# Spreading the state-space convolutions over linear-attention heads and gates, with deeper rings of decays

## The chip, the cores and the metric

The kernel runs on one core of one Trainium2 chip. The metric is the device time of one execution in microseconds (us). PE is the matrix engine, DVE the vector engine, ACT the scalar engine (it evaluates functions such as Exp, Ln and Silu and has to load a table of functions before it can use one that is not in the table it holds), POOL the third elementwise engine, and SP the queue from which most DMA transfers are issued. A verdict on this kernel can tell a change of about 0.2% from none, which is 4.9 us.

## The reference

Two layers of a hybrid encoder trunk on 512 tokens of width 1024, in float32. Each layer projects the normalised input with one wide matrix and feeds three mixers, whose outputs are gated and added:

```python
xbc = silu(dwconv_centred(xbc, conv_w, conv_b))          # 5 taps over the tokens: xs (1024), B and C (2 groups x 128)
y_f = ssd_chunked(xs, dtf, -exp(a_log_f), Bm, Cm)        # decay = exp(tril(a_i - a_j)), 16 heads of 64, chunks of 128
y_b = rev(ssd_chunked(rev(xs), rev(dtb), -exp(a_log_b), rev(Bm), rev(Cm)))
y   = rms_grouped((y_f + y_b + xs * d) * silu(z)) * norm_w
...
g_f = log_sigmoid(ga_f @ a2_f + bias_f) / 16             # linear attention: 4 heads, keys 128, values 256
o   = gla_chunked(q, k, v, g_f) + rev(gla_chunked(rev(q), rev(k), rev(v), rev(g_b)))
...
mixed = sig(gate0) * (y @ Ws) + sig(gate1) * (o @ Wg) + sig(gate2) * (na @ Wn)
x = x + mixed @ w_out;   x = x + relu(rms(x) @ w_ff1)^2 @ w_ff2
```

## The kernel before

All weights come as 128x1024 tiles, called granules here. For each granule SP issues a DMA into `wr`, ACT rounds it into a high part `wh` (L285), DVE subtracts for the low part `wl` (L287), and PE makes 24 matmuls of 512 columns (L304 high x high, L305 low x high, L306 high x low, for 8 slices) into a PSUM tile `pf`; value projections use two granules and tiles `pt` of 256 columns (L321 to L323). `wr`, `wh` and `wl` have rings of three, `pf`/`pt` one of two: a granule can start only when the one of the two tiles that it is given has been read out (evacuated) by DVE or ACT. A list of weight keys fixes the order of granules, and it must be the order in which the code asks for them. Within that order a scheduler places the instructions of each engine; every engine then runs its own list strictly in order.

Each layer has these stages: neighbourhood attention (N), linear attention (G), state-space (S), then the output projection and the MLP (F). The change touches G and S.

- G, four heads. `gla_proj(h)` makes values and gates (`gvg`), `q` and `k`. `gla_mix(h)` computes the decays for two directions d: a small matmul `ga` (L667), on ACT Abs, Exp and Ln (L670, L673, L674), on POOL a subtraction (L676), on DVE a scan (L682), on ACT two Exp of the scan (L685, L686) and one of a difference (L692), on DVE products with q and k (L693 to L699), and then the score matmuls `at` on PE (L709, L712). `gla_out` transposes a head's output (L780) and splits it into `Ah` (ACT L348) and `Al` (DVE L349). Branch granules `br_1x` (weights `br`, branch 1) multiply all eight `Ah`/`Al`; gate granules `gate_1x` make sigmoid gates (evacuated by L603, then ACT L605), and the branch's evacuation multiplies into the gate tile `gl` (L617).
- A convolution, `conv_tile`, is one granule (`xs`, `B` or `C`), its evacuation into `cu` on DVE (L789), one ACT pass (L792), four DVE passes (L797), and Silu on ACT (L798). Group 0 has six (xs_0 to xs_3, B_0, C_0), made after the last head has been projected; group 1 has six more.
- S, eight pairs of heads. For each head two rows of logarithmic decays are broadcast by DMA to 128 partitions (`S_E` and `S_eB`, 256 KB each); DVE takes differences and minima (L910), ACT scales two copies (`S_T`, `S_tb`, L912, L913) and takes Exp (L915), and DVE adds and multiplies (L916, L917). PE then multiplies (L945 into `S_py`, L956). Between the steps of a pair, `fill` runs granules of a list `todo`: the group 1 convolutions, gates and branches of branch 1, then z gates.

Of the kernel before, what the change touches and what calls it, by code (L numbers as in the profile page):

```python
# [199 lines left out]
def trunk(tc, a, out, layers=L, dbg=None):  # L200
    nc = tc.nc
    V, S, G, T = nc.vector, nc.scalar, nc.gpsimd, nc.tensor
    with ExitStack() as ctx:
# [13 lines left out]
        def nm(s):  # L217
            cnt[0] += 1
            return f"{s}_{cnt[0]}"
# [13 lines left out]
        def flat(ap):  # L233
            return ap.rearrange("p a b -> p (a b)")
# [20 lines left out]
        ph = Phase(tc, "F0", F_SB, F_PS)  # L255
# [41 lines left out]
        def feat(l, key, rh, rl, ps=None):  # L297

            hi, lo = wget(l, key)
            if ps is None:  # L300
                ps = psm("pf")
            for k in range(KT):
                c = slice(P * k, P * (k + 1))
                T.matmul(ps, lhsT=hi[:, c], rhs=rh[k], start=k == 0, stop=False)  # L304
                T.matmul(ps, lhsT=hi[:, c], rhs=rl[k], start=False, stop=False)  # L305
                T.matmul(ps, lhsT=lo[:, c], rhs=rh[k], start=False, stop=k == KT - 1)  # L306
            return ps
# [74 lines left out]
        for l in range(layers):  # L382
# [7 lines left out]
            ks = [("nk", t) for t in range(8)]  # L390
            for t in range(8):
                ks += [("nq", t), ("nv", t)]
            gk_ = lambda h: [("gvg", h, i) for i in range(4)] + [("gq", h), ("gk", h)]
            bk_ = lambda b, js=range(8): [k for j in js for k in (("gate", b, j), ("br", b, j))]
            ck_ = lambda g: [("xs", 4 * g + j) for j in range(4)] + [("B", g), ("C", g)]
            ks += [("sm", 0)] + gk_(0) + bk_(0) + gk_(1) + gk_(2) + gk_(3)
            ks += ck_(0) + ck_(1) + bk_(1) + [("z", j) for j in range(8)]
            ks += [("gate", 2, j) for j in range(5)]
            for j in range(8):
                ks += [("br", 2, j)] + ([("gate", 2, j + 5)] if j < 3 else [])  # L400
# [18 lines left out]
            if l:  # L419
                for j in range(KT):  # L420
# [5 lines left out]
            ph = Phase(tc, f"N{l}", {"s": 5, "pT": 4, "va0": (1, 1152), "va1": (1, 1152), "vb0": (1, 896), "vb1": (1, 896),  # L426
# [172 lines left out]
            def gate(b, j):  # L599
                ps = feat(l, ("gate", b, j), xh, xl)  # L600
                g_ = evac("gl")
                with hp():
                    V.tensor_tensor(g_, ps, rbc, ALU.mult)  # L603
                with hp():
                    S.activation(g_, g_, AF.Tanh, scale=0.5)  # L605
                return g_

            def branch(b, j, bh, bl, g_=None):
                if g_ is None:
                    g_ = gate(b, j)  # L610
                ps = feat(l, ("br", b, j), bh, bl)
                with hp():
                    if b == 0:
                        mixed[j] = pa.tile([P, NT], F32, tag="mix", name=nm("mixed"))
                        V.scalar_tensor_tensor(mixed[j], g_, 1.0, ps, ALU.add, ALU.mult)
                    else:
                        V.scalar_tensor_tensor(g_, g_, 1.0, ps, ALU.add, ALU.mult)  # L617
                if b:
                    G.tensor_tensor(mixed[j], mixed[j], g_, ALU.add)


            px_ = Phase(tc, f"X{l}", {"xs": 4, "bc": 2}, {})
            ph = Phase(tc, f"G{l}", {"A": 1, "kwT": 2, "st0": (3, 256), "st1": (3, 256), "t1": 3, "t2": 3, "w": 2,
                                     "gvg": 8, "bs": 2, "gst": 1, "q": 1, "k": 1, "a2": (2, 256), "kx": (2, 256)},
                       {"ga": 1, "at": 1, "x": 2, "po": 2})
# [9 lines left out]
            def gla_proj(h):  # L635
                v_, g_ = [], []
                for n, (r_, fn) in enumerate(((v_, AF.Copy), (g_, AF.Silu))):
                    ps = token(l, [("gvg", h, 2 * n), ("gvg", h, 2 * n + 1)], xh, xl)
                    for i in range(2):
                        t_ = ph.t("gvg", (P, 2, 256))  # L640
                        for b in (0, 1):
                            with hp():
                                S.activation(t_[:, b], ps[i][:, 256 * b: 256 * b + 256], fn,
                                             scale=rtok[:, 2 * i + b: 2 * i + b + 1])
                        r_.append(t_)
                ps = feat(l, ("gq", h), xh, xl)
                q_ = ph.t("q")
                with hp():
                    V.scalar_tensor_tensor(q_, ps, DK ** -0.5, rbc, ALU.mult, ALU.mult)
                ps = feat(l, ("gk", h), xh, xl)  # L650
                k_ = ph.t("k")
                with hp():
                    V.tensor_tensor(k_, ps, rbc, ALU.mult)
                return q_, k_, v_, g_
# [121 lines left out]
            def gla_out(g_):  # L776
                for vh in range(2):
                    py = ph.p("x", (P, 4, P))
                    for i in range(4):
                        T.transpose(py[:, i], g_[i // 2][:, i % 2, P * vh: P * (vh + 1)], ident)  # L780
                    h_, l_ = split(flat(py), cc(C_GLAN + vh), "Ah", "Al", pa)
                    glh.append(h_)
                    gll.append(l_)

            def conv_tile(pxs, n, i, ci):
                ps = feat(l, (n, i), xh, xl)
                u = evac("cu")
                with hp():
                    V.tensor_tensor(u, ps, rbc, ALU.mult)  # L789
                o = (px_ if n == "C" else pxs).t("xs" if n == "xs" else "bc")  # L790
                w_ = lambda k: cc(C_CW + 5 * ci + k)
                S.activation(o, u, AF.Identity, bias=cc(C_CB + ci), scale=w_(2))  # L792
                for k in (0, 1, 3, 4):
                    d = k - 2
                    so = slice(max(0, -d), NT - max(0, d))
                    si = slice(max(0, d), NT - max(0, -d))
                    V.scalar_tensor_tensor(o[:, so], u[:, si], w_(k), o[:, so], ALU.mult, ALU.add)  # L797
                S.activation(o, o, AF.Silu)  # L798
                return o

            conv_list = lambda g: [("xs", 4 * g + j, 4 * g + j) for j in range(4)] + [("B", g, 8 + g), ("C", g, 10 + g)]
# [3 lines left out]
            for j in range(8):  # L805
                branch(0, j, nah, nal)
            gla_out(y0)
            cur = gla_proj(1)
            for h in range(1, 4):
                y = gla_mix(h, *cur)  # L810
                if h < 3:
                    cur = gla_proj(h + 1)
                    gla_out(y)
            c0 = [conv_tile(px_, *k) for k in conv_list(0)]
            gla_out(y)
            ph.close()


            ph = Phase(tc, f"S{l}", {"xt": 2, "bt": 1, "gs": 1, "xw": (2, 768), "st": (2, 768), "eb": 4, "E": 4, "eB": 2,
                                     "T": 2, "tb": 1, "sm": 2, "xs": 4, "bc": 1, "tm": (1, 256)},  # L820
                       {"x": 4, "py": 2})

            pdt = ph.p("x", (P, 4, 32))
# [3 lines left out]
            sm = [smt[i // 4][:, i % 4].rearrange("p (c h) -> p c h", c=4) for i in range(8)]  # L827
# [161 lines left out]
                    sdl.append(l_)  # L989


            c1, todo = [], []
            for k in conv_list(1):
                todo.append(lambda k=k: c1.append(conv_tile(ph, *k)))
            for j in range(8):
                todo.append(lambda j=j: gls.append(gate(1, j)))
                todo.append(lambda j=j: branch(1, j, glh, gll, gls.pop(0)))
            for j in range(4):
                todo.append(lambda j=j: gate_tile(0, j, c0[:4]))
            gls = []  # L1000

            def fill(n=1):
                for _ in range(min(n, len(todo))):
                    todo.pop(0)()
# [5 lines left out]
            st = pair_states(0, 0, bts[0], cur[1])  # L1010
            for n, (g, j) in enumerate(pairs):
                nxt = pairs[n + 1] if n < 7 else None
                if nxt:
                    if nxt == (1, 0):
                        bts.append(ssd_group(1, c1))
                    new = pair_prep(*nxt, cs[nxt[0]])
                fill(1 + (n > 3))
                pair_out(g, j, cs[g], cur[0], cur[2], st)
                fill(1)
                if nxt:  # L1020
                    st = pair_states(*nxt, bts[nxt[0]], new[1])
                    cur = new
                fill(1)
# [7 lines left out]
            gs = [gate(2, j) for j in range(5)]  # L1031
# [6 lines left out]
            ph = Phase(tc, f"F{l + 1}", F_SB, F_PS)  # L1038
# [47 lines left out]
```

## Time and profile before

| | us |
|---|---|
| median of 3 runs (lowest, highest) | 2444.17 (2443.42, 2446.34) |
| the profiled execution, its own time | 2445.34 |
| its span, first to last instruction | 2443.6 |
| PE busy | 2428.9 (99%) |
| DVE busy | 1435.6 (59%) |
| ACT busy | 1157.9 (47%) |
| POOL busy | 393.3 (16%) |

PE is busy nearly all the time, so a time in this kernel is the work of PE and the gaps in it. The mean granted clock was 1.000, that is the 2.4 GHz level throughout. G of layer 0 lies at about 268 to 550 us and S at 550 to 700 us; S of layer 1 lies at about 1770 to 1910 us.

### The profile page before, as it was taken

What the parts mean: (1) busy time and instruction counts of PE and PEld (TensorE: products, weight loads), DVE (VectorE), ACT (ScalarE), POOL (GpSimd) and SP (SyncE); (2) the same over time, 40 slices, a digit from 0 to 9 for tenths busy, and PEclk for the clock granted to TensorE, in tenths of its full rate; (3) what the DMA queues carried; (4) which work ended last, traced back from release to release, by engine and by line L of the source; (5) the groups of instructions that cost most, each with busy time, mean ns of one, the idle gap of its engine ahead of it and who ended that gap; (6) DMA issues with size and microseconds to landing.
All of it is one profiled execution on the core that took longest, in us unless ns stands there. A gap on an engine that the chain in (4) does not pass through costs nothing.

```text
span 2443.6 us, 32635 instructions
## 1 busy us (share of the span) xinstructions
PE 2428.9 (99%) x12656; PEld 2063.0 (84%) x12656; DVE 1435.6 (59%) x2156; ACT 1157.9 (47%) x2055; POOL 393.3 (16%) x333
## 2 busy tenths in 40 slices
PE   9999999999999999999999999999999999999999
PEld 7899889987888888888888998899888888888887
DVE  6786534587976553443457755345989665534443
ACT  4475425556855342332335754265578543422321
POOL 3132101112431210000122321011134212100000
PEclk9999999999999999999999999999999999999999
DMA  5231222224533323223333222222245332232222
GB/s 183 89 105 63 90 87 79 72 77 134 166 112 126 100 96 97 95 95 100 124 125 97 86 69 88 87 73 85 78 139 168 102 129 95 95 100 98 93 97 87
DMA packets 84603, 249.38 MB, mean 102 GB/s; under 512 B 9824, under 2 KB 15840, under 8 KB 84448
## 3 DMA queue, kind: packets, MB, share of 16 engines
q1 hardware_dynamic: 84016, 246.85, 30.8%
q8 instruction: 100, 1.64, 0.3%
q10 hardware_dynamic: 432, 0.45, 0.1%
q14 instruction: 55, 0.45, 0.1%
HBM read 242.80 MB, written 4.46 MB: 101 GB/s over the span
## 4 chain that ended last, share of the span: by engine, by line
PE 96%; DMA 1%; DVE 1%; ACT 1%; issue 0%; SPq 0%; DVEq 0%
PE pf L305 14%; PE pf L304 14%; PE pf L306 14%; PE F_pf L304 11%; PE F_pf L306 11%; PE F_pf L305 11%; PE pt L322 3%; PE pt L323 3%; PE pt L321 3%; PE N_po L580 2%; PE N_pt L570 1%; PE S_x L956 1%; PE S_py L945 1%; PE N_sc L554 1%; PE N_sc L555 1%; PE G_x L743 1%
## 5 line engine op out<-in xcount | busy, mean ns | idle before, releaser
L285 ACT ACTIVATE wh<-wr 128x1024 fp32r<-128x1024 f32 x378 | 400.3, 1059 | 926.4 <-PE F_pf L305 429.7
L287 DVE TENSOR_TENSOR wl<-wr,wh 128x1024 fp32r<-128x1024 f32 x378 | 486.8, 1288 | 179.0 <-ACT wh L285 177.0
L304 PE MATMUL pf<-xh,wh 128*128 128x512 f32 x1232 | 485.6, 395 | 6.7 <-DVE gl L603 3.8
L305 PE MATMUL pf<-xl,wh 128*128 128x512 f32 x1232 | 486.3, 395 | 0.2 <-DVE xl L349 0.2
L306 PE MATMUL pf<-xh,wl 128*128 128x512 f32 x1232 | 485.1, 394 | 0.0
L304 PEld LDWEIGHTS pf<-xh,wh 128*128 128x128 f32 x1232 | 232.2, 189 | 57.1 <-DVE gl L603 4.6
L306 PEld LDWEIGHTS pf<-xh,wl 128*128 128x128 f32 x1232 | 232.1, 188 | 49.2 <-issue 1.5
L305 PEld LDWEIGHTS pf<-xl,wh 128*128 128x128 f32 x1232 | 232.1, 188 | 47.9 <-DVE xl L349 0.9
L304 PE MATMUL F_pf<-Ah,wh 128*128 128x512 f32 x640 | 248.3, 389 | 0.0
L305 PE MATMUL F_pf<-Al,wh 128*128 128x512 f32 x640 | 247.7, 389 | 0.0
L306 PE MATMUL F_pf<-Ah,wl 128*128 128x512 f32 x640 | 247.7, 389 | 0.0
L306 PE MATMUL F_pf<-xh,wl 128*128 128x512 f32 x512 | 200.0, 391 | 0.0
L305 PE MATMUL F_pf<-xl,wh 128*128 128x512 f32 x512 | 199.2, 389 | 0.0
L304 PE MATMUL F_pf<-xh,wh 128*128 128x512 f32 x512 | 199.2, 389 | 0.0
L1063 DVE TENSOR_TENSOR F_x<-F_x,F_pf 128x512 f32<-128x512 f32 x64 | 44.0, 687 | 206.7 <-PE F_pf L306 206.7
L322 PE MATMUL pt<-wl,xh 128*128 128x256 f32 x512 | 146.2, 286 | 0.0
L321 PE MATMUL pt<-wh,xh 128*128 128x256 f32 x512 | 145.4, 285 | 0.0
L323 PE MATMUL pt<-wh,xl 128*128 128x256 f32 x512 | 144.9, 284 | 0.0
L306 PEld LDWEIGHTS F_pf<-Ah,wl 128*128 128x128 f32 x640 | 120.1, 188 | 25.0
L305 PEld LDWEIGHTS F_pf<-Al,wh 128*128 128x128 f32 x640 | 120.2, 188 | 24.9
L304 PEld LDWEIGHTS F_pf<-Ah,wh 128*128 128x128 f32 x640 | 120.1, 188 | 24.9
L1056 DVE SCALAR_TENSOR_TENSOR F_v<-F_pf,rx 128x512 f32<-128x512 f32 x64 | 44.1, 691 | 159.6 <-PE F_pf L306 159.5
(315 smaller groups left out, 4243.0 us busy)
## 6 DMA issues: line engine op xcount, KB each, us to landing
wr<-pk SPq DMA_DIRECT2D x378, 512.0 KB, 3.3
N_bias<-bias SPq DMA_DIRECT2D x48, 256.0 KB, 2.8
S_E<-acd SPq DMA_DIRECT2D x32, 256.0 KB, 4.4
S_eB<-acd SPq DMA_DIRECT2D x32, 256.0 KB, 3.7
S_eb<-ead SPq DMA_DIRECT2D x64, 96.0 KB, 3.6
F_x<-xt SPq DMA_DIRECT2D x15, 256.0 KB, 5.4
xd<-F_x SPq DMA_DIRECT2D x8, 256.0 KB, 2.0
F_x<-xd SPq DMA_DIRECT2D x8, 256.0 KB, 5.5
```

The lines of the kernel that those rows point to most:

```text
L285: S.activation(hi, raw, AF.Copy)
L287: V.tensor_tensor(lo, raw, f(hi), ALU.subtract)
L304: T.matmul(ps, lhsT=hi[:, c], rhs=rh[k], start=k == 0, stop=False)
L305: T.matmul(ps, lhsT=hi[:, c], rhs=rl[k], start=False, stop=False)
L306: T.matmul(ps, lhsT=lo[:, c], rhs=rh[k], start=False, stop=k == KT - 1)
L321: T.matmul(o, lhsT=rh[k][:, s], rhs=hi[:, c], start=k == 0, stop=False)
L322: T.matmul(o, lhsT=rh[k][:, s], rhs=lo[:, c], start=False, stop=False)
L323: T.matmul(o, lhsT=rl[k][:, s], rhs=hi[:, c], start=False, stop=k == KT - 1)
L554: T.matmul(sc[:, i], lhsT=q_[hh][:, qs], rhs=kh[hh][:, kr], start=True, stop=False)
L580: T.matmul(po[:, P * cb: P * (cb + 1)], lhsT=z_[:, c: c + P], rhs=pts[hh][:, i, kb], start=hh + kb == 0, stop=hh + kb == 2)
L1056: V.scalar_tensor_tensor(v_, ps, 0.0, rbc, ALU.max, ALU.mult)
L1063: V.tensor_tensor(xT[j], xT[j], ps, ALU.add)
```

## The change

The xs_0 and xs_1 convolutions of group 0 move to the place between head 0's output and head 1's projection. xs_2 moves to the place between head 2's projection (with head 1's output) and head 2's mix. xs_3, B_0 and C_0 stay after head 3's mix is emitted. In S the six convolutions of group 1 no longer stand first in `todo` but alternate with gates and branches. `fill(1 + (n > 3))` becomes `fill(1)`, so each pair gets three granules. The rings of E, eB and tb grow from 4, 2 and 1 to 5, 3 and 2 tiles. The number of instructions is the same on PE, DVE, POOL and SP; ACT's list has 83 table loads in place of 75. Lines of the changed kernel lie one further down in G, and four further down in S.

```diff
@@ the list of weight keys
-            ks += [("sm", 0)] + gk_(0) + bk_(0) + gk_(1) + gk_(2) + gk_(3)
-            ks += ck_(0) + ck_(1) + bk_(1) + [("z", j) for j in range(8)]
+            ks += [("sm", 0)] + gk_(0) + bk_(0) + ck_(0)[:2] + gk_(1) + gk_(2) + ck_(0)[2:3] + gk_(3) + ck_(0)[3:]
+
+            ks += [k for p in zip(ck_(1), bk_(1)) for k in p] + bk_(1)[6:] + [("z", j) for j in range(8)]
@@ stage G
             gla_out(y0)
+            c0 = [conv_tile(px_, *k) for k in conv_list(0)[:2]]
             cur = gla_proj(1)
             for h in range(1, 4):
                 y = gla_mix(h, *cur)
                 if h < 3:
                     cur = gla_proj(h + 1)
                     gla_out(y)
-            c0 = [conv_tile(px_, *k) for k in conv_list(0)]
+                if h == 1:
+                    c0.append(conv_tile(px_, *conv_list(0)[2]))
+            c0 += [conv_tile(px_, *k) for k in conv_list(0)[3:]]
             gla_out(y)
@@ stage S
-            ph = Phase(tc, f"S{l}", {"xt": 2, "bt": 1, "gs": 1, "xw": (2, 768), "st": (2, 768), "eb": 4, "E": 4, "eB": 2,
-                                     "T": 2, "tb": 1, "sm": 2, "xs": 4, "bc": 1, "tm": (1, 256)},
+            ph = Phase(tc, f"S{l}", {"xt": 2, "bt": 1, "gs": 1, "xw": (2, 768), "st": (2, 768), "eb": 4, "E": 5, "eB": 3,
+                                     "T": 2, "tb": 2, "sm": 2, "xs": 4, "bc": 1, "tm": (1, 256)},
@@
-            c1, todo = [], []
-            for k in conv_list(1):
-                todo.append(lambda k=k: c1.append(conv_tile(ph, *k)))
+            c1, gls, todo = [], [], []
             for j in range(8):
                 todo.append(lambda j=j: gls.append(gate(1, j)))
                 todo.append(lambda j=j: branch(1, j, glh, gll, gls.pop(0)))
+            for i, k in enumerate(conv_list(1)):
+                todo.insert(2 * i, lambda k=k: c1.append(conv_tile(ph, *k)))
...
-                fill(1 + (n > 3))
+                fill(1)
```

The first place is head 2 of G, on ACT. `G0_t1_113` and `G0_t2_114` are the decay tiles of direction 0, `G0_t1_116` that of direction 1, `X0_xs_5` of the changed kernel is the tile of the xs_2 convolution, and `wh_451` the weights of the next value granule. Before:

```order
L670 ACTIVATE G0_t1_113_4244<-G0_ga_112_4242,col_1_120 128x512
L329 ACT_TABLE_LOAD
L673 ACTIVATE G0_t1_113_4244<-G0_t1_113_4244 128x512
L674 ACTIVATE G0_t1_113_4244<-G0_t1_113_4244 128x512
L643 ACTIVATE G0_gvg_146_4503<-pt_438_4405,tcol_91_648 128x256 x2
L670 ACTIVATE G0_t1_116_4254<-G0_ga_115_4252,col_1_120 128x512
L685 ACTIVATE G0_t1_113_4244<-G0_bs_118_4261 128x512
L686 ACTIVATE G0_t2_114_4245<-G0_bs_118_4261 128x512
L673 ACTIVATE G0_t1_116_4254<-G0_t1_116_4254 128x512
L692 ACTIVATE G0_w_119_4267<-G0_w_119_4267 128x512
L674 ACTIVATE G0_t1_116_4254<-G0_t1_116_4254 128x512
```

In the changed kernel, from the second Abs on:

```order
L671 ACTIVATE G0_t1_116_4374<-G0_ga_115_4372,col_1_120 128x512
L644 ACTIVATE G0_gvg_146_4623<-pt_453_4525,tcol_91_648 128x256 x2
L674 ACTIVATE G0_t1_116_4374<-G0_t1_116_4374 128x512
L799 ACT_TABLE_LOAD
L799 ACTIVATE X0_xs_5_4350<-X0_xs_5_4350 128x512
L675 ACT_TABLE_LOAD
L675 ACTIVATE G0_t1_116_4374<-G0_t1_116_4374 128x512
L686 ACT_TABLE_LOAD
L686 ACTIVATE G0_t1_113_4364<-G0_bs_118_4381 128x512
L687 ACTIVATE G0_t2_114_4365<-G0_bs_118_4381 128x512
L693 ACTIVATE G0_w_119_4387<-G0_w_119_4387 128x512
L285 ACTIVATE wh_451_4521<-wr_450_4519 128x1024
```

The Exp of direction 0 (L686, before L685) stood ahead of the Exp and Ln of direction 1 and now stands behind them, behind the Silu of xs_2 and behind three table loads; the rounding of `wh` follows it as before. Layer 1 has the same order with its own numbers. On DVE the scan of direction 1 (L683 into `G0_bs_121`) now stands between two products of direction 0 (L700 and L699); before, it stood behind them.

The second place is the end of G, on PE. `pf_521_5495` of the changed kernel is the tile of br_10, `pf_530` of gate_11 and `pf_535` of xs_7; `pf_521_5501` of before is the tile of xs_7 and `pf_526` of B_1. Before:

```order
L825 MATMUL S0_x_15_5145<-con_116,gtmp_117 128x32 x4
L304 MATMUL pf_521_5501<-xh_20_178,wh_509_5314 128x512
L305 MATMUL pf_521_5501<-xl_21_179,wh_509_5314 128x512
L306 MATMUL pf_521_5501<-xh_20_178,wl_510_5315 128x512
L304 MATMUL pf_521_5501<-xh_22_182,wh_509_5314 128x512
L305 MATMUL pf_521_5501<-xl_23_183,wh_509_5314 128x512
L306 MATMUL pf_521_5501<-xh_22_182,wl_510_5315 128x512
L304 MATMUL pf_526_5558<-xh_8_154,wh_514_5429 128x512
```

In the changed kernel:

```order
L829 MATMUL S0_x_15_5145<-con_116,gtmp_117 128x32 x4
L305 MATMUL pf_521_5495<-Al_501_5120,wh_509_5314 128x512
L306 MATMUL pf_521_5495<-Ah_500_5119,wl_510_5315 128x512
L304 MATMUL pf_530_5643<-xh_22_182,wh_519_5491 128x512
L305 MATMUL pf_530_5643<-xl_23_183,wh_519_5491 128x512
L306 MATMUL pf_530_5643<-xh_22_182,wl_520_5492 128x512
L304 MATMUL pf_535_5705<-xh_8_154,wh_523_5541 128x512
```

The last two matmuls of br_10 now come only three matmuls ahead of xs_7, which takes the same PSUM tile. On DVE the evacuation of br_10 (L618 into `gl_512`) stands here, behind the low part of the last `Ah` and a row of convolution passes:

```order
L349 SCALAR_TENSOR_TENSOR Al_501_5120<-G0_x_191_5114,col_1_120,Ah_500_5119 128x512
L798 SCALAR_TENSOR_TENSOR S0_xs_36_5305<-cu_507_5303,col_1_120,S0_xs_36_5305 128x510
L798 SCALAR_TENSOR_TENSOR S0_xs_53_5454<-cu_517_5452,col_1_120,S0_xs_53_5454 128x510
L798 SCALAR_TENSOR_TENSOR S0_xs_36_5305<-cu_507_5303,col_1_120,S0_xs_36_5305 128x511
L287 TENSOR_TENSOR wl_524_5542<-wr_522_5539,wh_523_5541 128x1024
L798 SCALAR_TENSOR_TENSOR S0_xs_53_5454<-cu_517_5452,col_1_120,S0_xs_53_5454 128x511
L798 SCALAR_TENSOR_TENSOR S0_xs_64_5572<-cu_526_5570,col_1_120,S0_xs_64_5572 128x510
L798 SCALAR_TENSOR_TENSOR S0_xs_36_5305<-cu_507_5303,col_1_120,S0_xs_36_5305 128x511
L798 SCALAR_TENSOR_TENSOR S0_xs_53_5454<-cu_517_5452,col_1_120,S0_xs_53_5454 128x511
L835 TENSOR_TENSOR S0_sm_16_5150<-S0_x_15_5145,col_1_120 128x128
L798 SCALAR_TENSOR_TENSOR S0_xs_64_5572<-cu_526_5570,col_1_120,S0_xs_64_5572 128x511
L618 SCALAR_TENSOR_TENSOR gl_512_5343<-gl_512_5343,pf_521_5495 128x512
```

Ahead of the first row stand L349 into `Al_499` and the evacuation of xs_6 (L790). Before, the same stretch of DVE held convolution evacuations and passes, with no `gl` among them:

```order
L797 SCALAR_TENSOR_TENSOR S0_xs_54_5460<-cu_517_5458,col_1_120,S0_xs_54_5460 128x510
L797 SCALAR_TENSOR_TENSOR S0_xs_36_5305<-cu_507_5303,col_1_120,S0_xs_36_5305 128x511
L797 SCALAR_TENSOR_TENSOR S0_xs_37_5345<-cu_512_5343,col_1_120,S0_xs_37_5345 128x511
L831 TENSOR_TENSOR S0_sm_16_5150<-S0_x_15_5145,col_1_120 128x128
L797 SCALAR_TENSOR_TENSOR S0_xs_54_5460<-cu_517_5458,col_1_120,S0_xs_54_5460 128x511
L797 SCALAR_TENSOR_TENSOR S0_xs_36_5305<-cu_507_5303,col_1_120,S0_xs_36_5305 128x510
L789 TENSOR_TENSOR cu_522_5526<-pf_521_5501,rx_25_213 128x512
L797 SCALAR_TENSOR_TENSOR S0_xs_37_5345<-cu_512_5343,col_1_120,S0_xs_37_5345 128x510
```

The tile of xs_7 (`cu_522`) was read out two passes behind the dt matmul's L831, and the granule that waits for that tile came 24 matmuls later.

## Rows read from the trace of the kernel before

**Rows 1.** page of the profile: span; PE busy us, share, instructions

```profile
span 2443.6 us, 32635 instructions
...
PE 2428.9 (99%) x12656; PEld 2063.0 (84%) x12656; DVE 1435.6 (59%) x2156; ACT 1157.9 (47%) x2055; POOL 393.3 (16%) x333
```

**Rows 2.** waits of PE, whole span: us in total, times, longest

```profile
PE pf L304 <- DVE gl L603: 3.8, 2, 2.1
```

**Rows 3.** stretches: busy us of each engine, clock, DMA share, GB/s

```profile
400.00:450.00 50.00, 50.00 (x357) 46.92 (x356) 24.84 (x47) 27.31 (x43) 5.99 (x5) 1.00 0.23 76
600.00:650.00 50.00, 47.53 (x289) 38.25 (x288) 46.45 (x90) 39.40 (x111) 19.47 (x16) 1.00 0.63 192
650.00:700.00 50.00, 49.55 (x279) 41.36 (x278) 45.80 (x76) 38.40 (x107) 22.30 (x17) 1.00 0.49 146
1800.00:1850.00 50.00, 48.35 (x285) 39.54 (x284) 43.23 (x81) 45.09 (x122) 17.10 (x13) 1.00 0.64 185
1850.00:1900.00 50.00, 49.45 (x297) 40.95 (x296) 48.20 (x80) 38.17 (x107) 24.37 (x20) 1.00 0.52 158
```

**Rows 4.** timeline of PE, first head pair: start, duration, idle before, releaser

```profile
609.69 0.50 PE L304 MATMUL pf<-xh,wh 128*128 128x512 f32 x1 [2.12 <-DVE gl L603]
```

**Rows 5.** timeline of DVE, the same place

```profile
598.43 1.14 DVE L910 SCALAR_TENSOR_TENSOR S_E<-S_E,S_sm,S_eB 128x128 f32<-128x128 f32 x4 [2.69 <-DMA S_eB<-acd]
...
601.51 1.14 DVE L910 SCALAR_TENSOR_TENSOR S_E<-S_E,S_sm,S_eB 128x128 f32<-128x128 f32 x4 [1.34 <-DMA S_eB<-acd]
...
608.96 0.68 DVE L603 TENSOR_TENSOR gl<-pf,rx 128x512 f32<-128x512 f32 x1
```

**Rows 6.** timeline of ACT, attention head 2 of layer 0

```profile
445.98 1.28 ACT L329 ACT_TABLE_LOAD   x1
447.27 0.63 ACT L673 ACTIVATE G_t<-G_t 128x512 f32<-128x512 f32 x1
...
450.26 0.84 ACT L643 ACTIVATE G_gvg<-pt,tcol 128x256 f32<-128x256 f32 x2 [1.69 <-PE pt L323]
...
451.56 0.64 ACT L685 ACTIVATE G_t<-G_bs 128x512 f32<-128x512 f32 x1
```

**Rows 7.** timeline of PE, the same head

```profile
443.99 0.47 PE L667 MATMUL G_ga<-G_gst,G_a 96*128 96x512 f32 x1
...
450.06 0.40 PE L667 MATMUL G_ga<-G_gst,G_a 96*128 96x512 f32 x1
...
457.49 1.00 PE L709 MATMUL G_at<-G_t,G_t 128*128 128x64 f32 x8
```

**Rows 8.** timeline of DVE, the same head

```profile
449.97 1.22 DVE L682 TENSOR_TENSOR_SCAN G_bs<-con,G_t 128x512 f32<-128x512 f32 x1 [2.50 <-POOL G_t L676]
...
454.75 1.52 DVE L698 TENSOR_TENSOR G_t<-G_w,G_k 128x256 f32<-128x256 f32 x1
```

**Rows 9.** timeline of ACT, attention head 1 of layer 0

```profile
401.66 1.28 ACT L674 ACT_TABLE_LOAD   x1
...
405.15 1.28 ACT L685 ACT_TABLE_LOAD   x1
```

**Rows 10.** timeline of PE, end of the attention stage of layer 0

```profile
548.27 0.39 PE L304 MATMUL pf<-xh,wh 128*128 128x512 f32 x1
548.50 1.03 PE L780 MATMUL G_x<-con,G_gvg 128*128 128x128 f32 x8
```

**Rows 11.** timeline of ACT, the same place

```profile
549.35 1.27 ACT L348 ACTIVATE Ah<-G_x,col 128x512 fp32r<-128x512 f32 x2 [2.77 <-PE G_x L780]
550.51 1.51 ACT L792 ACTIVATE S_xs<-cu,col 128x512 f32<-128x512 f32 x2
```

**Rows 12.** timeline of DVE, the same place

```profile
550.07 1.41 DVE L349 SCALAR_TENSOR_TENSOR Al<-G_x,col,Ah 128x512 fp32r<-128x512 f32 x2 [0.87 <-ACT Ah L348]
...
554.03 1.22 DVE L287 TENSOR_TENSOR wl<-wr,wh 128x1024 fp32r<-128x1024 f32 x1
555.17 2.73 DVE L797 SCALAR_TENSOR_TENSOR S_xs<-cu,col,S_xs 128x511 f32<-128x511 f32 x4
```

More of the change, by code (lines that the diff above doesn't have):

```diff
@@ L997, in trunk @@
                 todo.append(lambda j=j: branch(1, j, glh, gll, gls.pop(0)))
+            for i, k in enumerate(conv_list(1)):
+                todo.insert(2 * i, lambda k=k: c1.append(conv_tile(ph, *k)))
             for j in range(4):
                 todo.append(lambda j=j: gate_tile(0, j, c0[:4]))
-            gls = []
             def fill(n=1):
```

## The prediction

> **What bounds the kernel now.** I read the page first: PE is busy for 2428.9 us of a span of 2443.6 us [rows 1], so no more than 14.7 us can be won without taking matmuls away, and the change takes none away. The waits of PE come next [rows 2]. The largest is for the evacuation of gates by DVE, 3.8 us in 2 pieces, and the reader sees that it belongs to work that DVE owes PE. The stretches of 50 us place them [rows 3]: in G PE has no gap (400 to 450 us: 50.00 us busy), in S of layer 0 it lacks 2.47 + 0.45 us, in S of layer 1 1.65 + 0.55 us, together 5.1 us. In the same rows DVE is busy for 43 to 48 of 50 us, against 24.8 us in G. The timelines of the worst place show why [rows 4, 5]: the granule at 609.69 us waited 2.12 us for the gate evacuation at 608.96 us, which stood in DVE's list behind decay work that had itself waited 2.69 and 1.34 us for broadcasts of `S_eB`.
>
> **The change part by part.** *Deeper rings and fewer granules per pair, in S.* With three `S_eB` tiles the second and third broadcast can be issued beside the first, and the wait of 1.34 us goes. That of 2.69 us stays: it is for the first pair of broadcasts, which is issued at the same place as before. Against this, the Silu of C_1 now falls on ACT between the exponentials of the first and the second head, with a table load on either side (a load takes 1.28 us and an ACT pass over such a tile 0.63 us, [rows 6], so 2 x 1.28 + 0.63 = 3.2 us). The bounds are 0 and the whole 5.1 us of both layers; late pairs never made PE wait, so taking granules from them gives nothing by itself. I take 2.0 us, the wait that goes (1.34 us) and part of the 2.12 us behind it, since the order leaves the gate evacuation behind four groups of decay work. What is late next in S is the same thing, DVE's list.
>
> *xs_0 and xs_1 between heads 0 and 1; xs_3, B_0 and C_0 as before.* Same granules, same evacuations, one more table load; no attention chain runs on ACT there, since head 1's starts two projections later. Cost 0; the cover is the projection of `gvg`, 96 matmuls of 0.12 us = 11.5 us, and without it the load would cost 1.28 us.
>
> *xs_2 ahead of head 2's mix.* This is the largest term. Take t = 0 at the first `ga` matmul, 443.99 us before [rows 7]. The scores `at` followed at 457.49, t = 13.50: the second `ga` at 450.06, and in between 108 value matmuls of 0.12 us (60 of them in the last 7.2 us). In the changed kernel there are 109, so `at` is due at 13.6. Before, the Exp of direction 0 (L685) began at 451.56, t = 7.6 [rows 6], and the last product that `at` needs (L698) ended at 454.75 + 1.52 = 456.27, t = 12.3 [rows 8]: 1.2 us to spare.
> Now follow ACT in the new order. Abs ended at 445.98, t = 2.0, behind two splits; now one rounding of `wh` stands ahead of it, and I leave it at 2.0. A load, 1.28 [rows 6], 3.3; the convolution's pass, 0.75 (two in 1.51, [rows 11]), 4.0; Exp and Ln at 0.65 each, 5.3. The second `ga` is made at 6.1 [rows 7], so Abs waits for it and ends at 6.8; the evacuation of a value tile, 0.84 less some overlap, 7.5; Exp 8.15; then load 9.4, Silu, taken like an Exp, 10.1, load 11.4, Ln 12.0, load 13.3. Only here does the Exp of direction 0 start, 5.7 us later than before, though its scan was done near 7.7. From that Exp to the end of L698 it took 4.7 us before, of which about 1.1 us was a slow L698 (1.52 us for 256 columns beside a busy POOL, where L603 took 0.68 us for 512, [rows 5]). In the changed order POOL is idle then, but a scan of 1.22 us [rows 8] stands in between: Exps and difference to 15.0, product and scan to 17.0, the last product to 17.4. `at` starts 17.4 - 13.6 = 3.8 us late. Behind it on PE stands everything else, so the gap is lost; on ACT the rounding of the next `wh`, due at 13.5 as well, follows the difference at 15.0 and hides in the same gap. The bounds are 0 (the loads lie in time in which ACT would have idled) and 5.7 us (the whole delay of the Exp). I take 3.9 us in each layer, 7.8 us in both.
> A rule bears on this. The Trainium skill, "ScalarE: Activation LUTs", section "Rules for kernel authors", says to do all the work of one table set before switching to another; the change goes against it at this place. The section "What ACT_TABLE_LOAD costs" prices a switch at about 2.66 us, a load of 1.28 us and a drain of 1.38 us. Here the load took 1.28 us and Exp started 0.01 us after it (445.98 + 1.28 = 447.26, [rows 6]), so the trace shows no drain on top, and the sum goes by 1.28 us. By 2.66 us, an estimate from that page, the three loads would add 4.1 us more in each layer.
>
> *The end of G.* xs_7 gets the PSUM tile of br_10, whose last matmuls now wait for the output of head 3. Take T = 0 at the first of the eight transposes (L780, [rows 10]). Before, ACT made `Ah` from T = 0.85 (549.35 - 548.50) to 2.1, DVE `Al` from 1.57 to 2.98 [rows 11, 12]. Now three matmuls of xs_6 end at 1.5, br_10's fourth-last group starts at 1.6, its `Al` matmul waits for `Al` until 2.4: 0.55 us. gate_11 needs the evacuation of xs_6, which stands behind that `Al` and ends near 2.95: 0.1 us more. gate_11's 21 matmuls (0.23 us each, [rows 10]), the dt matmuls and br_10's last two end at 8.5, and xs_7 is due three matmuls later, at 9.2. But DVE, after the second `Al` at 3.6, has eight convolution passes of 0.68 us (2.73 for four), one `wl` of 1.13 (1.22 less overlap, [rows 12]) and a short L835, taken as 0.25: 3.6 + 5.4 + 1.1 + 0.25 = 10.35, and then the evacuation itself, 0.68: 11.0. xs_7 starts 1.8 us late. Sum 2.5 us in each layer, 5.0 us in both. The lower bound is 0.7 us a layer, if the passes run ahead of my count so that only the `Al` waits stay; the upper is 3.0 us, with half a microsecond for passes slowed by POOL, as L698 was.
>
> **Sum.** 7.8 + 5.0 - 2.0 = +10.8 us. It is made against the profiled execution, 2445.34 us, which lies 1.17 us over the median of 2444.17 us; the same step from the median gives **2455.0 us**. A change under 0.2% (4.9 us) cannot be told from none.
>
> **The rivals.**
> 1. Head 2 stalls, the end of G does not, since DVE reaches br_10's evacuation in time: 2444.2 + 7.8 - 2.0 = 2450.0 us. For it: DVE is only half busy in G [rows 3]. Against: its list is in order, and the passes stand ahead.
> 2. The end of G stalls, head 2 does not: 2444.2 + 5.0 - 2.0 = 2447.2 us, same. For it: in head 1 two loads stand in direction 1's chain at 401.66 and 405.15 us [rows 9] and PE had no gap between 400 and 450 us [rows 3]. Against: there the Exp of direction 0 stood ahead of them; in head 2 it stands behind.
> 3. Neither stalls, S gives its 2.0 us: 2442.2 us, same.
> 4. On the other side, faster: broadcasts alone made S wait, the third `S_eB` tile frees DVE before the gate evacuations, all 5.1 us come back and neither new gap appears: 2439.1 us, 5.1 us less, just past the bound. It decides if the gate evacuation of the first pair ends before PE gets there, 2.1 us sooner than at 608.96. Against: the first wait, 2.69 us, does not depend on the ring.
> 5. A switch between sets costs about twice its row when it interrupts a running chain, three more loads of 1.28 us in each layer: 2455.0 + 2 x 3.8 = 2462.7 us. Against: Exp followed its load by 0.01 us [rows 6]. The page on the LUTs named above is the one that would have it so; by its price, an estimate, it would be 2463.2 us.
>
> **How the numbers follow.** The forecast has 0.64 (own range 2450 to 2460), rival 1 0.12, rival 2 0.11, rival 3 0.07, rival 4 0.03, rival 5 0.03. The bounds of the terms give 2444.2 + 11.4 + 6.0 - 0 = 2461.6 us at the top. The range of 2446 to 2460 us leaves out rivals 3 to 5 and the upper corner. Slower is the forecast with rivals 1 and 5, 0.79; same is rivals 2 and 3, 0.18; faster is rival 4, 0.03.
>
> **What would show it.** In the changed profile PE must wait some 4 us at L710 of head 2 in both layers, released by DVE (the product L699) or by ACT, with the three loads close together on ACT ahead of L686. At the end of G PE must wait for a gate tile `gl` written at L618, just ahead of xs_7, 1 to 2 us, and 0.5 us for `Al` just before. In S the wait for L604 must shrink but not vanish, and DVE must wait for `S_eB` once in place of twice. I am wrong if PE is gapless in head 2: then ACT's lateness was hidden; or if a gap appears in S that no row of before has, which would make it slower by a way not counted here.

## The result, and the profile after

| | before | after |
|---|---|---|
| median on the same chip, us (5 runs each) | 2445.65 (2443.42 to 2446.94) | 2464.87 (2463.40 to 2466.32) |
| ratio, 95% interval | | 1.0079 (1.0066 to 1.0093) |
| span of the profiled execution, us | 2443.6 | 2461.6 |
| mean granted clock | 1.000 | 0.998 |

The change made the kernel 19.2 us slower. The forecast was +10.8 us with a range that ended at 2460 us: the sign was right, the size was not. Of the executions in this study, one each of e4 (6059 us), e15 (2681 us) and the kernel before (3474 us) ran far slower than the rest; they move no median by more than 0.2 us, and the ratios leave them out. The page of the changed kernel has the same work on PE as before [rows 1], 6.7 us longer, and a span 18.0 us longer:

```profile
span 2461.6 us, 32655 instructions
...
PE 2435.6 (99%) x12656; PEld 2065.5 (84%) x12656; DVE 1435.7 (58%) x2156; ACT 1166.3 (47%) x2063; POOL 399.9 (16%) x333
```

The waits of PE (total, times, longest) answer to [rows 2]. The wait for a gate at L603 is gone; in its place stand others, above all these:

```profile
PE S_x L960 <- DVE S_st L939: 5.7, 10, 1.1
PE pt L321 <- ACT wh L285: 4.3, 2, 2.2
PE G_at L710 <- DVE G_t L699: 2.2, 2, 1.1
PE pf L304 <- DVE gl L618: 2.2, 2, 1.1
...
PE pf L304 <- ACT Ah L345: 0.7, 2, 0.4
...
PE pf L305 <- DVE Al L349: 0.6, 2, 0.3
```

**Head 2.** The timeline of PE, where [rows 7] stood before:

```profile
473.37 0.28 PE L323 MATMUL pt<-wh,xl 128*128 128x256 f32 x1
475.82 0.39 PE L321 MATMUL pt<-wh,xh 128*128 128x256 f32 x1 [2.17 <-ACT wh L285]
477.30 1.19 PE L710 MATMUL G_at<-G_t,G_t 128*128 128x64 f32 x8 [1.09 <-DVE G_t L699]
...
480.06 0.41 PE L323 MATMUL pt<-wh,xl 128*128 128x256 f32 x1
480.27 0.41 PE L321 MATMUL pt<-wh,xh 128*128 128x256 f32 x1
...
481.81 0.28 PE L323 MATMUL pt<-wh,xl 128*128 128x256 f32 x1
481.93 0.28 PE L321 MATMUL pt<-wh,xh 128*128 128x256 f32 x1
```

Value matmuls follow each other at 0.12 us. From 473.37 to 475.82 us is 2.45 us, so 2.33 us are lost for `wh`; L710 comes 1.36 us later than it would follow that matmul. Together 3.69 us, and the same 2.33 and 1.36 us in layer 1. What the forecast did not have stands behind the gap: at 480 us the same matmuls come 0.21 us apart. Two short stretches of the clock, one in each layer (PE busy, PEld, DVE, ACT and POOL busy, then the clock), show it:

```profile
478.50:481.50 3.00, 3.00 (x17) 2.88 (x18) 3.00 (x6) 0.37 (x1) 2.59 (x1) 0.50 0.70 186
...
1700.50:1703.50 3.00, 3.00 (x18) 2.88 (x19) 3.00 (x6) 0.42 (x1) 2.55 (x1) 0.50 0.60 190
```

The granted clock was 0.50, the 1.2 GHz level in place of 2.4, from 478.2 to 481.6 us; in 3.4 us PE did the work of 1.7. Before, the clock was at 1.00 here [rows 3]. The ACT timeline of the same place, against [rows 6]:

```profile
467.31 0.64 ACT L674 ACTIVATE G_t<-G_t 128x512 f32<-128x512 f32 x1
467.97 1.28 ACT L799 ACT_TABLE_LOAD   x1
469.26 0.63 ACT L799 ACTIVATE X_xs<-X_xs 128x512 f32<-128x512 f32 x1
469.91 1.28 ACT L675 ACT_TABLE_LOAD   x1
471.21 0.63 ACT L675 ACTIVATE G_t<-G_t 128x512 f32<-128x512 f32 x1
471.86 1.28 ACT L686 ACT_TABLE_LOAD   x1
473.15 0.63 ACT L686 ACTIVATE G_t<-G_bs 128x512 f32<-128x512 f32 x1
...
474.73 1.04 ACT L285 ACTIVATE wh<-wr 128x1024 fp32r<-128x1024 f32 x1
```

The three loads stand as forecast, and Silu started 0.01 us behind the first one's end (467.97 + 1.28 = 469.25). The section "What ACT_TABLE_LOAD costs" of the Trainium skill's "ScalarE: Activation LUTs" adds a drain of 1.38 us to each; the trace does not agree, as before the change.

**The end of G**, on PE and then on DVE, against [rows 10, 12]:

```profile
567.22 0.50 PE L305 MATMUL pf<-Al,wh 128*128 128x512 f32 x1 [0.29 <-DVE Al L349]
...
575.78 0.47 PE L304 MATMUL pf<-xh,wh 128*128 128x512 f32 x1 [1.10 <-DVE gl L618]
```

```profile
571.45 2.73 DVE L798 SCALAR_TENSOR_TENSOR S_xs<-cu,col,S_xs 128x511 f32<-128x511 f32 x4
574.10 0.28 DVE L835 TENSOR_TENSOR S_sm<-S_x,col 128x128 f32<-128x128 f32 x1
574.30 0.74 DVE L798 SCALAR_TENSOR_TENSOR S_xs<-cu,col,S_xs 128x511 f32<-128x511 f32 x1
574.96 0.68 DVE L618 SCALAR_TENSOR_TENSOR gl<-gl,pf 128x512 f32<-128x512 f32 x1
```

By the usual distance of such neighbours PE lost 0.56 and 1.26 us here (0.56 and 1.24 in layer 1): xs_7 started as soon as DVE, behind its row of passes, had read br_10's tile.

**S.** A wait that no row of before has. DVE, and then PE:

```profile
624.22 2.30 DVE L914 SCALAR_TENSOR_TENSOR S_E<-S_E,S_sm,S_eB 128x128 f32<-128x128 f32 x4
626.44 0.68 DVE L921 TENSOR_TENSOR S_E<-S_E,S_T 128x512 f32<-128x512 f32 x1
627.04 0.41 DVE L938 TENSOR_TENSOR S_tm<-S_st,S_sm 128x256 f32<-128x256 f32 x1
...
627.95 0.43 DVE L938 TENSOR_TENSOR S_tm<-S_st,S_sm 128x256 f32<-128x256 f32 x1
628.29 1.22 DVE L287 TENSOR_TENSOR wl<-wr,wh 128x1024 fp32r<-128x1024 f32 x1
629.43 0.41 DVE L939 TENSOR_TENSOR S_st<-S_st,S_tm 128x256 f32<-128x256 f32 x1
```

```profile
629.90 1.16 PE L960 MATMUL S_x<-X_bc,S_st 128*128 128x128 f32 x8 [0.52 <-DVE S_st L939]
```

PE waits for the running state, whose update (L938, L939) stands in DVE's list behind decay groups (L914) of other heads and behind the low part of a granule (L287, 1.22 us).

**The account of the profiled 18.0 us**, from the distances of PE's neighbours: gap in head 2 +7.4, lower clock +3.4, end of G +3.6. In S the pieces over 0.2 us were 3.16 and 2.42 us in the two layers before; they are 3.58 and 2.99 now, +1.0. The rest, 2.6 us, is spread: a wait for `Ah` (L345) behind S took 0.52 us in each layer where 0.24 us were lost before, and the others are pieces under 0.2 us. The profiled execution is the fastest of the five, at a mean clock of 0.998; the other four had 0.996 to 0.997, so they spent more time at the lower level.

### The profile page after: what moved, and what is told of

Read it like the earlier page. It is cut to its first block, busy times and chain, and to the rows that moved or that the text cites. A ratio compares the mean times of both kernels' runs of the same rounds, so it can differ in the third digit from the quotient of the medians.

```text
span 2461.6 us, 32655 instructions
## 1 busy us (share of the span) xinstructions
PE 2435.6 (99%) x12656; PEld 2065.5 (84%) x12656; DVE 1435.7 (58%) x2156; ACT 1166.3 (47%) x2063; POOL 399.9 (16%) x333
## 4 chain that ended last, share of the span: by engine, by line
PE 92%; DVE 4%; DMA 1%; ACT 1%; issue 1%; SPq 0%; DVEq 0%
PE pf L304 14%; PE pf L305 14%; PE pf L306 14%; PE F_pf L304 11%; PE F_pf L305 11%; PE F_pf L306 11%; PE N_po L581 2%; PE pt L321 2%; PE pt L322 2%; PE pt L323 2%; PE N_pt L571 1%; DMA S_E<-acd 1%; DVE S_E L914 1%; PE N_sc L555 1%; PE N_sc L556 1%
## 5 line engine op out<-in xcount | busy, mean ns | idle before, releaser
L287 DVE TENSOR_TENSOR wl<-wr,wh 128x1024 fp32r<-128x1024 f32 x378 | 485.7, 1285 | 171.8 <-ACT wh L285 169.9
```

Source lines behind the costliest of these rows:

```text
L287: V.tensor_tensor(lo, raw, f(hi), ALU.subtract)
```

## The experiments

Each kernel ran 5 rounds beside the kernel before on the same chip (e11: 3). "Over before" is the difference of the two medians.

| kernel | median us | over before | ratio, interval |
|---|---|---|---|
| e2 only xs_2 moved | 2465.66 | +19.9 | 1.0080 (1.0067 to 1.0093) |
| e1 changed kernel, xs_2 back | 2449.55 | +3.5 | 1.0016 (1.0007 to 1.0024) |
| e13 only xs_0, xs_1 moved | 2451.02 | +5.0 | 1.0023 (1.0014 to 1.0032) |
| e5 changed kernel, Silu of xs_2 late | 2460.26 | +14.5 | 1.0058 (1.0044 to 1.0072) |
| e14 changed kernel, xs_2 behind mix 2 | 2462.60 | +16.5 | 1.0068 (1.0056 to 1.0081) |
| e11 changed kernel, gap filled | 2464.13 | +18.1 | 1.0073 (1.0059 to 1.0087) |
| e6 changed kernel, br_10 later | 2471.22 | +25.2 | 1.0105 (1.0089 to 1.0120) |
| e10 e1 and e6 together | 2453.14 | +7.1 | 1.0032 (1.0020 to 1.0045) |
| e3 only the rings | 2447.62 | +1.9 | 1.0007 (0.9998 to 1.0016) |
| e4 changed kernel, old rings | 2469.37 | +23.6 | 1.0095 (1.0079 to 1.0110) |
| e7 all of S, nothing of G | 2446.52 | +0.5 | 1.0001 (0.9993 to 1.0010) |
| e12 e7 with old rings | 2453.45 | +7.4 | 1.0029 (1.0018 to 1.0041) |
| e15 e7 with the old `fill` | 2444.79 | -0.5 | 0.9998 (0.9989 to 1.0007) |

**Where the time lies: xs_2 alone (e2), taken back (e1), and xs_0, xs_1 alone (e13).** The edits are one line of the list each, with the matching calls. Against before, e2 has `gk_(2) + ck_(0)[2:3] + gk_(3)` and nothing else; against the changed kernel, e1 has

```diff
-  ... + gk_(1) + gk_(2) + ck_(0)[2:3] + gk_(3) + ck_(0)[3:]
+  ... + gk_(1) + gk_(2) + gk_(3) + ck_(0)[2:]
-                if h == 1:
-                    c0.append(conv_tile(px_, *conv_list(0)[2]))
-            c0 += [conv_tile(px_, *k) for k in conv_list(0)[3:]]
+            c0 += [conv_tile(px_, *k) for k in conv_list(0)[2:]]
```

e13 has, against before, `bk_(0) + ck_(0)[:2] + gk_(1)` and the other four convolutions where they were.

> The kernel before with only the xs_2 convolution of group 0 moved ahead of head 2's mix. Theory (this move alone makes the gap of 3.7 us and the low clock behind it, per layer): 2445.7 + 10.4 = 2456 us, three table loads on ACT ahead of the Exp of direction 0. Rival (the gap needs the other edits too): 2446 to 2449 us.

> The changed kernel with the xs_2 convolution of group 0 back behind head 3's mix. Theory (the move of xs_2 makes a gap of 3.7 us in head 2 and, by that gap, a stretch at the lower clock that costs 1.7 us, in each layer, whatever the gap comes from): no gap and no low clock in head 2, 2464.9 - 10.8 = 2454.1 us. Rival (the gap moves to head 3, where xs_2 then stands): above 2460 us, PE waiting in head 3.

> Only xs_0 and xs_1 moved to the place between heads 0 and 1. Prediction's step (cost 0): 2445.7 us, same as before within 1 us. Rival (their two granules are missing as cover later, and all that follows in G and S moves by two granules): 1 to 3 us more, 2447 to 2449 us, with new waits of PE at the end of G or in S and none in heads 0 and 1.

xs_2 alone costs as much as the whole change, and about twice what I had expected of it. e2 has the same 2.33 + 1.36 us in each layer, and the clock was at 0.50 for twice as long in each (3.41 us lost). That is 14.2 us; the other 5.7 us lie in S, where PE waits for `S_E` and `S_st`. With xs_2 back all three G terms vanish, the wait at the end of G too, so the move of xs_2 is worth 19.2 - 3.5 = 15.7 us in the changed kernel: the gap at the end of G needs it too. The prediction gave xs_0 and xs_1 no cost; e13 shows 5.0 us, more than its rival's 1 to 3 us. Its waits of PE:

```profile
PE S_py L946 <- DVE S_E L918: 3.8, 4, 1.1
PE S_x L877 <- DVE S_eb L958: 2.8, 2, 1.4
...
PE S_x L957 <- DVE S_st L936: 1.6, 3, 0.7
```

All three lie in S, none at heads 0 and 1, so the cover named for the load held and the cost fell elsewhere. In e13's order PE is one granule further down the list when S begins (at the dt matmuls), and 205 large matmuls stand between these and the first `S_py`, 188 before the change: granules that fed S's first pairs now fill the time in which head 3 is finished, and everything in S meets DVE's list at another moment. That this makes the waits is argued from the order; no run isolates it.

**Head 2: the loads, the place of the code, the clock (e5, e14, e11).** e5 leaves all of the changed kernel and puts the Silu of xs_2 on ACT behind head 2's copies of `kwT`; e14 writes the convolution behind head 2's mix, at the same place in the list of weights; e11 adds three matmuls of 512 columns, whose result is not used, where PE idled:

```diff
# e5
-                S.activation(o, o, AF.Silu)
+                if not late:
+                    S.activation(o, o, AF.Silu)
...
+                if h == 2:
+                    with tc.issue_after(kins[0].ins):
+                        S.activation(c0[2], c0[2], AF.Silu)
# e14
                 y = gla_mix(h, *cur)
+                if h == 2:
+                    c0.append(conv_tile(px_, *conv_list(0)[2]))
...
-                if h == 1:
-                    c0.append(conv_tile(px_, *conv_list(0)[2]))
# e11
+                    if h == 2 and d == 0:
+                        dm = ph.p("ga")
+                        for _ in range(3):
+                            T.matmul(dm[0:8], lhsT=e_, rhs=rst, start=True, stop=True)
```

> The changed kernel with one order edge more: the Silu of xs_2 is queued on ACT behind head 2's copies of its transposed keys, so that it no longer stands between Exp and Ln of direction 1. Theory (table loads in head 2's chain make PE wait 3.7 us in each layer, and the clock falls because of that gap and costs about 1.5 us more): PE has no gap at L710 or ahead of it, the granted clock of that stretch is 1.00, and the time is 2464.9 - 2 x 5.2 = 2454.5 us. Rival 1 (the granule's place by itself delays the weights of gvg_33): the gap stays above 2 us and the time above 2460 us. Rival 2 (the low clock is not the gap's doing): the gap goes, the low clock stays, 2457.5 us.

> The changed kernel with the xs_2 granule at the same place in the list of weights (between the projections of heads 2 and 3), but its convolution written behind head 2's mix in place of ahead of it. Theory (the gap in head 2 and the low clock behind it come from where the convolution is written, since that lets its ACT and DVE work pass ahead of the chain of direction 0): no wait at L710 in head 2, granted clock 1.00 there, the end of G as in the changed kernel (1.8 us per layer), so 2464.9 - 2 x 3.7 - 3.4 = 2454 us. Rival (the granule's place in the list is enough, whatever is written first): the gap stays over 2 us per layer, 2461 to 2466 us.

> The changed kernel with three extra matmuls (8x512 in float32, their result unused) in each layer, released by the first decay column of head 2, which PE makes in the gap of 3.7 us. Theory (the idle time of PE brings the lower clock behind it): PE's idle piece in head 2 shrinks to about 1.7 us, the granted clock stays 1.00 in both layers' head 2, time 2461 to 2464 us though the added work is not useful. Rival (the lower clock comes from something else at that place): clock 0.50 for 3.4 us in each layer as in the changed kernel, 2465 us or more.

In e5 the loads were gone from the chain, yet PE still lost 2.58 us in head 2 of each layer, so the loads are not the whole cause, and the numbers of rival 1 came out. Its longest waits of PE there, and what stood on DVE:

```profile
PE pt L322 <- DVE wl L287: 4.8, 2, 2.4
```

```profile
465.79 4.04 DVE L800 SCALAR_TENSOR_TENSOR X_xs<-cu,col,X_xs 128x510 f32<-128x510 f32 x4 [0.82 <-ACT X_xs L795]
...
474.26 1.21 DVE L685 TENSOR_TENSOR_SCAN G_bs<-con,G_t 128x512 f32<-128x512 f32 x1
475.39 0.40 DVE L698 TENSOR_TENSOR G_t<-G_t,G_k 128x256 f32<-128x256 f32 x1
475.71 1.26 DVE L700 TENSOR_TENSOR G_kx<-G_t,G_k 128x256 f32<-128x256 f32 x1
476.89 1.21 DVE L287 TENSOR_TENSOR wl<-wr,wh 128x1024 fp32r<-128x1024 f32 x1
```

The four passes of xs_2 stand ahead of the scan of direction 0, which began at 470.42 us, though POOL had finished its input at 468.49 us. The low part of the next value granule stands behind the products of direction 0 and the scan of direction 1. With e14 the two loads around Silu moved into the chain of direction 1, and PE waited there instead (`wh` 1.5 us a layer, then L710; about 2.4 us lost in all). So its theory fell and its rival came out, in the gap and in the time: not the order of the text, but that a Silu and a granule of DVE and ACT work lie between two heads, makes PE wait for one or the other chain. Only leaving xs_2 out of this place (e1) took the gap away.

The clock followed the gap. e11 against e14, stretches over head 2 of the two layers:

```profile
470.00:490.00 20.00, 18.03 (x137) 15.11 (x136) 13.03 (x27) 13.14 (x19) 7.52 (x5) 1.00 0.15 53
1690.00:1712.00 22.00, 20.15 (x154) 17.22 (x154) 14.25 (x29) 15.23 (x23) 6.15 (x6) 1.00 0.14 49
```

```profile
470.00:490.00 20.00, 17.73 (x117) 16.55 (x116) 11.85 (x25) 9.96 (x13) 3.09 (x2) 0.83 0.16 53
1690.00:1712.00 22.00, 19.73 (x156) 18.64 (x155) 16.21 (x33) 10.87 (x16) 4.28 (x3) 1.00 0.15 48
```

With the gap cut by useless matmuls to pieces of 1.6 and 0.5 us, the clock stayed at 1.00 in both layers, and the mean clocks of e11's four executions are 0.999 to 1.000, where the changed kernel has 0.996 to 0.998. The time is 2464.13 us, just above the theory's range and only 1.1 us nearer to before than the changed kernel; the filler itself takes 2.74 us of PE in each layer. With pieces of 1.6 and 0.8 us and no filler (e14) it fell in layer 0 and not in layer 1; with one of 2.58 us (e5) in layer 1 alone. With 3.69 us (the changed kernel, e2, e4, e6) it fell in all eight layers, and 1.7 us were lost in five of them, 3.4 us in three. So PE's idle time is what brings it here, and the shorter gaps don't always do so. The Trainium skill, "TensorE: Matmul & The Clock Gate", section "Part 1: The HAM clock gate", says that the gate looks at PE's activity at a rhythm of its own, whatever the kernel does; one layer of two, in e5 and in e14, fits that, but no run here tests it.

**The end of G (e6, e10).** br_10 goes one place down the list, behind xs_6 (`todo[3], todo[4] = todo[4], todo[3]` and the same swap of the keys); e10 has e1's edit as well.

> The changed kernel with br_10 one place later in the list (behind xs_6). Theory (br_10 is asked for before head 3's output is there, which costs 0.56 + 1.26 us per layer at the end of G): these two waits go, 2464.9 - 3.6 = 2461.3 us; the gap of head 2 and its low clock stay. Rival (DVE is behind there in any order, and the next granule waits instead): within 1 us of the changed kernel.

> The changed kernel with xs_2 back behind head 3's mix and br_10 one place later. Theory (the two costs are independent): 2464.9 - 10.8 - 3.6 = 2450.5 us, which leaves the cost of S. Rival (they interact): more than 2 us off that.

Both are slower than the kernel without the swap (by 25.2 - 19.2 = 6.0 and 7.1 - 3.5 = 3.6 us): e6 lies outside its theory and its rival, and in e10 the rival came out. In e6 the wait for `Al` is gone, but the granule that takes br_10's tile still waits 1.31 us for its evacuation (`gl` L620), which again stands behind a row of passes, nine in 6.04 us. In S `S_py` now waits 3.6 us, where it had not waited, and the longest wait for a state is 2.1 us in place of 1.1. Behind these waits the clock fell in both layers:

```profile
622.00:625.00 3.00, 3.00 (x9) 2.35 (x8) 2.46 (x4) 1.76 (x7) 2.79 (x3) 0.50 0.94 282
1847.50:1850.50 3.00, 3.00 (x9) 2.33 (x8) 3.00 (x4) 1.66 (x6) 2.72 (x3) 0.50 0.94 283
```

Each stretch lasted 3.4 us and lost 1.7, so the two make 3.4 of the 7.4 us between the profiled spans of e6 and the changed kernel. e1 has no wait at the end of G, so in e10 the swap had nothing to remove there. That DVE's row of passes sets the gap at the end of G agrees with the changed kernel's timeline, but no run has taken the passes away alone.

**S (e3, e4, e7, e12, e15).** The three edits of S, one by one: rings (`"E": 5, "eB": 3, "tb": 2`), spread (`todo.insert(2 * i, ...)`), and `fill(1)` for `fill(1 + (n > 3))`. e3 is the rings alone, e7 all three without any move in G, e12 is e7 without the rings, e15 is e7 without the new `fill`, e4 the changed kernel without the rings.

> The kernel before with only the three rings deeper. Theory (the rings take away the wait of 2.3 us for the gate evacuation, and put decay work ahead of the state updates, which costs about as much): within 2 us of before, 2443.7 to 2447.7 us, with PE waiting for S_st. Rival 1 (the forecast's term): 2 to 5 us less, 2440.7 to 2443.7 us, no wait for S_st. Rival 2 (rings alone are worse): above 2448 us.

> The changed kernel with the old rings (E 4, eB 2, tb 1). Theory (rings made the waits of PE for S_st, 3.6 us per layer, and took away the waits for gates): the waits for S_st shrink under 1 us per layer, waits of DVE for S_eB come back, and the time is within 4 us of the changed kernel, 2461 to 2469 us. Rival (the spreading of granules made the waits for S_st): they stay at 3 us or more per layer and the time rises to 2468 us or more. Both: the gap in head 2 stays as it is.

> The edits of stage S alone (group 1 spread among gates and branches, three granules for each pair, deeper rings), with the group 0 convolutions where they were before. Theory (S itself became slower, since what is left of the 19 us after head 2 and the end of G is about 5 us): 2448 to 2452 us, PE waiting for S_st as in the changed kernel. Rival 1 (the rest comes from xs_0 and xs_1 in G): 2446 us or less. Rival 2 (the forecast's term): 2441 to 2444 us.

> Only the new order of the list in S (group 1 convolutions alternating with gates and branches) and three granules for each pair, old rings, group 0 at its old place. Theory (the spread removes the waits for gates, and the rings add nothing to that): S waits of PE under 1 us per layer, 2446 to 2447 us, as with the rings. Rival (the rings are what lets the spread work): waits of 2 us and more per layer for S_py, S_st or gl, 2448 to 2451 us.

> The new order of the list in S and the deeper rings, but with the old number of granules for each pair (three for early pairs, four for later ones); group 0 at its old place. Theory A (the extra 2.3 us of PE time of the S part come from three granules for each pair, which leaves more granules for the end and other changes between small and large matmuls): S waits under 1 us per layer as with all S edits, and the 2.3 us gone, 2443.5 to 2444.5 us, which would beat both kernels. Theory B (they come from the spread itself): 2446 to 2447 us.

e7's waits of PE in S are those of the gates alone:

```profile
PE pf L304 <- DVE gl L604: 0.9, 2, 0.6
```

In its profiled execution (2444.60 us, its fastest) the gaps in S fell by 3.1 us, inside the forecast's bounds, but the other distances of PE's neighbours add up to 2.3 us more, and the median did not fall: 2446.52 us, outside all three ranges. Where the 2.3 us come from is not shown. PE changes between granules and small matmuls (`S_py` and others) 68 times from the start of S to F in a layer, 64 before; but e3 changes 70 times and e15 72, and their distances grew by less. e12 shows that the spread needs the rings, against my expectation: without them DVE waits 9.1 us for `S_eB` and PE stands at

```profile
PE S_x L957 <- DVE S_st L936: 4.8, 4, 1.3
PE S_py L946 <- DVE S_E L918: 3.3, 3, 1.4
```

for 6.9 us more than e7. e4 agrees in the changed kernel: without the rings the waits for `S_st` are gone, but PE waits 3.0 us for gates and 2.4 us for `S_E`, and the time rises by 4.4 us, though 1.7 us near 40 us and 1.7 us in head 2 of its profile are the clock's. The rings alone (e3) change the gate wait from 3.8 [rows 2] to 2.1 us and put 2.9 us of state waits there; e3, e7 and e15 cannot be told from before. e15 leaves open whether the new `fill` eats e7's gain: its -0.5 against e7's +0.5 us is within the noise, its profiled execution, 2449.08 us, is one of two some 4 us above its median, and by that trace the waits in S are about 2 us in each layer, where theory A had under 1 us. No kernel of the study is faster than the one before.

## Why the prediction was wrong

- **PE as the bound, and the price of a gap.** Right: every gap of the account is lost time.
- **Head 2, 3.9 us a layer.** Right in size: 3.69 us (worked out as 3.8, taken as 3.9). The order of ACT came out as worked through, and `at` was late behind L699 (L698 before). The rounding of the next `wh` "hides in the same gap", as said: it ended the first 2.33 us, but L710, one value matmul further, was held by L699 in any case. What was off is the reason: the loads are not all of it (e5: 2.58 us without them), since the granule's own passes on DVE delay the same chain.
- **The clock.** This step failed: it is not in the sum at all, and cost 3.4 us. A gap was counted as its own length, while PE ran at 1.2 GHz behind it. e11 shows that with the gap filled this does not happen. Rival 5 stated an upper size near the result, 2462.7 us, for a reason that the trace denies: each load still ended 0.01 us ahead of the next pass.
- **The end of G, 2.5 us a layer.** Right in mechanism, 1.8 us in size: the `Al` wait 0.56 (forecast 0.55), xs_7 1.26 (forecast 1.8).
- **xs_0 and xs_1, "Cost 0".** This step failed. They cost 5.0 us with the old S (e13) and 2449.55 - 2446.52 = 3.0 us with the new one (e1 against e7). The text named the load and its cover, and counted the granules as moved work with no effect behind them. They had stood between head 3's projection and S; the list behind them moved up into that place, and e13's new waits lie in S.
- **S, -2.0 us.** This step failed too. DVE's waits for `S_eB` fell as said, in layer 0 from two, 4.0 us, to one of 2.3 us, and the wait for L604 is not only smaller but gone. But PE's pieces in S are 1.0 us more, not 2.0 less, by the way named as fatal in the last part of the prediction: a gap that no row of before has, at L960. Even with G as before, the edits of S give nothing that can be told from noise (e7): the gaps that went came back as longer distances elsewhere.

The failed steps carry 3.4 + (1.0 + 2.0) = 6.4 us of the profiled difference to the forecast, and the small pieces 2.6; the terms that came out smaller take back 0.4 and 1.4 us: 10.8 + 6.4 + 2.6 - 1.8 = 18.0 us. These terms go by place, so what xs_0 and xs_1 cost is inside S and the spread pieces, 1.0 + 2.6 = 3.6 us; e1, without any gap in G, is 3.5 us over before. What stays open: which neighbours make most of the 2.6 us, where e7's 2.3 us come from, and how e13's 5.0 us divide between the granules used early and the new order on DVE.

## What to carry to other kernels

A granule that is moved takes its cover along: ask what now fills the place that it left, and follow the list behind it, not only the place where it lands. On an engine that is nearly always busy, price a gap of some microseconds above its own length, since the clock may fall behind it. Where every engine runs its list strictly in order, a function of another table, and the rounding and passes that come with its granule, belong where no chain is running that PE will wait for.

## What was not expected of the hardware

The granted clock fell to 0.50 behind gaps of PE of 2.4 to 3.7 us, for stretches in which 1.7 or 3.4 us were lost, and equal gaps of 2.4 to 2.6 us brought it in one layer and not in the other (e5, e14). In six of the fifteen profiles (e1, e4, e5, e10, e11, e15) it also fell near 40 us, a place that no edit touches, and took 1.7 us there. It fell in S as well: in e6 at 622 and 1847 us, in e10 at 1832 us and in e15 at 1819 us, there behind two waits of 0.97 and 0.92 us. In eleven, the changed kernel among them, it fell at 8 to 11 us too, with no cost that shows in the changed kernel: its first matmul of G came at 263.9 us, before at 264.3. In the profile of the kernel before none of this happened.
